# Global heads of an encoder trunk: groups of four query blocks, and softmax tiles shared by two blocks

## The chip, the cores and the metric

The kernel runs on one core of a Trainium2 chip. The core has a matrix engine (TensorE, in the profile PE, with its weight loads as a row of their own, PEld), three engines that work on rows of 128 partitions (VectorE or DVE, ScalarE or ACT, GpSimd or POOL), and an engine that here only issues transfers (SyncE or SP). Matmul results land in PSUM, a memory of eight banks of 128 partitions by 512 float32 columns; everything else lives in SBUF. The metric is the device time of one launch in microseconds, the median of several runs.

## The reference, cut to what matters

Two encoder layers of width 1024 over 1024 tokens. The first layer has three kinds of heads side by side; the change touches the kind with global attention, 8 query heads of width 64 that share 2 key and value heads.

```python
def global_gqa(q, k, v):
    ...
    scale = dh ** -0.5
    qb = q.reshape(B, nb, BLOCK, Hkv, G, dh).transpose(1, 0, 2, 3, 4, 5)

    def one(qblk):
        s = jnp.einsum('bqkgd,bskd->bkgqs', qblk, k).astype(jnp.float32) * scale
        p = jax.nn.softmax(s, axis=-1).astype(v.dtype)
        return jnp.einsum('bkgqs,bskd->bqkgd', p, v)
```

For each head and each block of 128 queries: the scores against all 1024 keys, a softmax along the keys, and the product with the values. Everything is float32.

## The kernel before, in words

**Stages.** One program does both layers. The first layer's attention (the phase `l0`) runs four passes; the method `even` calls `global_pair` once in each, at about 142 to 480 us of the span. A pass holds two query heads (`i` = 0, 1) of one key and value head, so 2 x 8 blocks of 128 queries. The other work of a pass is memory attention (`mem_att`) behind `global_pair`, and projections of the layer's input that later heads and the gate need.

**Numbers in two parts.** Matmul operands are rounded to a shorter form, and what rounding loses is carried in a second operand: a high and a low part. Keys come as `kh` and `kl`. A score tile takes four matmuls of 512 columns: two halves of the keys, each with `kh` and `kl` (L1046, L1047).

**A block's softmax.** `scores(i, g, b)` makes it: four matmuls into a PSUM tile `sa` of two banks (two such tiles, so two blocks at once); the maximum on DVE (L1051); on ACT one exponential of 1024 columns into an SBUF tile `P`, whose sum is accumulated on the way and fetched by a second small instruction (L1052); the reciprocal on DVE (L1053); and on POOL the multiplication by it (L1054). There are six `P` tiles of 128 x 1024.

**A group.** Two blocks of one head form a group (`g` = 0 to 3). Their weights stand with queries in the partitions, and must be turned so that keys do: PE transposes 128 x 128 pieces ("flips", L133) into a PSUM tile `tr`, four at a time, two key chunks of 128 of both blocks. `p_parts` takes the high part out on ACT (`ph`, L125) and the low part, the difference, on DVE (`pl`, L549). Four value matmuls of 256 columns follow (L1080): for each of the two chunks the high and the low part, all adding up in the one PSUM tile `pv`. That happens four times in a group (`c` = 0, 2, 4, 6). The values carry their own two parts in the upper and lower 64 output rows; at the group's end ACT copies the lower rows out (`bt`) and DVE adds both (L1086) into the pass's output `yb`.

**What lies between.** `pull(n)` issues steps of put-off projections: one step is three matmuls of 512 columns on one PSUM tile `pj` (L242). One step follows each set of flips, and four follow each of the pass's first two scores. So PE does the projections while ACT and DVE work on the softmax. `next(side)` issues other sums on POOL. New scores (`todo`) are begun ahead of chunks 0 and 4, so a pass is two blocks ahead of the flips.

**What sets the order.** The program text sets only dependencies and priorities. A scheduler with its own time model then orders each engine's instructions; `ahead(kind)` moves an instruction forward by the number of places given for `l0`: score=20, exp=60, part=150, close=120. The kinds `flip` and `pv` have no number there. On the chip each engine works through its own fixed list, and waits by semaphores. A tile with n buffers makes its n+1st writer wait for the last reader of the first: `P` has 6, `sa` 2, `tr` 2, `pv` 1, `pj` 1, `ph` and `pl` 3 each.

## Time and profile before

| what | us |
|---|---|
| median of 3 runs | 1479.58 (1479.55 to 1482.57) |
| profiled execution, its own time | 1482.22 |
| its span, first to last instruction | 1480.4 |
| mean granted TensorE clock | 0.998 |
| flips, all of the kernel (L133), x752 | 115.3 busy |
| exponentials of the global heads (L1052), x64 | 71.5 busy on ACT |
| maxima of the global heads (L1051), x64 | 77.5 busy on DVE |
| normalisations of the global heads (L1054), x64 | 73.8 busy on POOL |

The profile is of one execution. A row of a group names the line, the engine, the operation and the tiles (out<-in); then its count, its busy time, the mean length of one, and how long the engine stood idle before it with what ended that. A row of the timeline gives start and length in us, and in brackets how long the engine had waited and for what. Lengths of matmuls overlap, since PE starts one while the one before still drains: what a matmul costs is the step from its start to the next one's start, not its length. ACT and DVE rows overlap a little in the same way.

### The profile page before, as it was taken

What the parts mean: (1) busy time and instruction counts of PE and PEld (TensorE: products, weight loads), DVE (VectorE), ACT (ScalarE), POOL (GpSimd) and SP (SyncE); (2) the same over time, 40 slices, a digit from 0 to 9 for tenths busy, and PEclk for the clock granted to TensorE, in tenths of its full rate; (3) what the DMA queues carried; (4) which work ended last, traced back from release to release, by engine and by line L of the source; (5) the groups of instructions that cost most, each with busy time, mean ns of one, the idle gap of its engine ahead of it and who ended that gap; (6) DMA issues with size and microseconds to landing.
All of it is one profiled execution on the core that took longest, in us unless ns stands there. A gap on an engine that the chain in (4) does not pass through costs nothing.

```text
span 1480.4 us, 24751 instructions
## 1 busy us (share of the span) xinstructions
PE 1461.3 (99%) x8049; PEld 1254.1 (85%) x8049; DVE 1038.8 (70%) x2125; ACT 839.2 (57%) x1877; POOL 647.0 (44%) x766
## 2 busy tenths in 40 slices
PE   9999999999999999999999999999999999999997
PEld 8898888888888888888888887888888888888776
DVE  6687777777776678776687866654457787778584
ACT  7743665556655466655454544444456777776454
POOL 1223658566775656553450000002425556665355
PEclk9999999999999999999999999999999999999999
DMA  8966335334342524378553343567675568778844
GB/s 282 314 161 184 117 114 168 122 122 132 117 144 79 199 75 139 110 263 313 182 180 135 136 136 139 156 171 256 225 257 169 187 198 270 246 250 313 306 132 150
DMA packets 171809, 271.87 MB, mean 184 GB/s; under 512 B 15648, under 2 KB 92704, under 8 KB 170656
## 3 DMA queue, kind: packets, MB, share of 16 engines
q1 hardware_dynamic: 171248, 270.20, 56.6%
q8 instruction: 64, 1.05, 0.3%
q14 instruction: 65, 0.53, 0.1%
q10 hardware_dynamic: 432, 0.09, 0.0%
HBM read 174.28 MB, written 83.89 MB: 174 GB/s over the span
## 4 chain that ended last, share of the span: by engine, by line
PE 87%; DMA 4%; DVE 4%; ACT 2%; issue 1%; SPq 1%; POOL 0%; DVEq 0%; ACTq 0%; POOLq 0%
PE pj L242 16%; PE pj L62 12%; PE x L1650 7%; PE tr L133 6%; PE pv L1080 4%; PE y L1650 4%; PE pv L62 3%; PE s L62 3%; PE sa L1348 3%; PE tr L62 3%; PE pj L1348 2%; PE pv L1650 2%; PE sa L1046 2%; PE sa L1047 2%; PE s L1348 2%; PE tr L1348 2%
## 5 line engine op out<-in xcount | busy, mean ns | idle before, releaser
L549 DVE TENSOR_TENSOR pl<-tr,ph 128x512 fp32r<-128x512 f32 (+2 forms) x352 | 204.3, 594 | 45.2 <-ACT ph L125 43.3
L242 PE MATMUL pj<-H,wh 128*128 128x512 f32 x704 | 233.4, 412 | 0.4 <-DVE vt L313 0.2
L125 ACT ACTIVATE ph<-tr 128x512 fp32r<-128x512 f32 (+2 forms) x352 | 176.8, 523 | 99.6 <-PE tr L133 77.8
L158 POOL TENSOR_SCALAR wh<-wraw 128x512 fp32r<-128x512 f32 x48 | 30.4, 636 | 268.0 <-PE x L1650 233.2
L125 ACT ACTIVATE wh<-wraw 128x384 fp32r<-128x384 f32 (+1 forms) x163 | 89.2, 554 | 98.5 <-PE pj L1348 11.8
L242 PE MATMUL pj<-H,wl 128*128 128x512 f32 x352 | 139.0, 395 | 0.0
L242 PEld LDWEIGHTS pj<-H,wh 128*128 128x128 f32 x704 | 120.2, 189 | 18.2 <-issue 0.6
L62 PE MATMUL pj<-H,wh 128*128 128x512 f32 x384 | 121.0, 396 | 0.0
L1133 POOL TENSOR_SCALAR pn<-pn,st 128x384 f32<-128x384 f32 (+1 forms) x128 | 72.9, 572 | 99.3 <-DVE st L1132 57.5
L133 PE MATMUL tr<-ident,P 128*128 128x128 f32 x752 | 115.3, 273 | 0.8 <-DVE pl L549 0.5
L1295 POOL TENSOR_TENSOR wl<-wraw,wh 128x384 fp32r<-128x384 f32 x56 | 63.5, 1135 | 89.7 <-ACT wh L125 78.7
L1131 ACT ACTIVATE pn<-pn,st 128x384 f32<-128x384 f32 (+1 forms) x128 | 75.1, 587 | 40.4 <-DVE st L1128 38.9
L133 PEld LDWEIGHTS tr<-ident,P 128*128 128x128 f32 x752 | 88.8, 140 | 9.5 <-DVE pl L549 1.8
L1052 ACT ACTIVATE P<-sa,st 128x1024 f32<-128x1024 f32 x64 | 71.5, 1117 | 34.4 <-DVE st L1051 16.9
L1054 POOL TENSOR_SCALAR P<-P,st 128x1024 f32<-128x1024 f32 x64 | 73.8, 1155 | 27.5 <-DVE st L1053 27.2
L1051 DVE TENSOR_REDUCE st<-sa 128x1 f32<-128x1024 f32 x64 | 77.5, 1218 | 8.0 <-PE sa L1047 7.4
L62 PE MATMUL s<-k,q 128*128 128x384 f32 (+1 forms) x352 | 81.4, 327 | 0.7 <-DMA k<-k 0.7
L242 PEld LDWEIGHTS pj<-H,wl 128*128 128x128 f32 x352 | 66.2, 188 | 15.2
L62 PE MATMUL pj<-H,wl 128*128 128x512 f32 x192 | 75.6, 394 | 0.0
L160 POOL TENSOR_TENSOR wl<-wraw,wh 128x512 fp32r<-128x512 f32 x52 | 71.3, 1373 | 9.6 <-ACT wh L125 7.2
L62 PEld LDWEIGHTS pj<-H,wh 128*128 128x128 f32 x384 | 66.6, 188 | 5.4
L864 PE MATMUL pj<-ah,H 128*128 128x256 f32 x384 | 70.7, 282 | 0.3 <-ACT ah L125 0.2
(574 smaller groups left out, 4170.0 us busy)
## 6 DMA issues: line engine op xcount, KB each, us to landing
y<-yb SPq DMA_DIRECT2D x24, 512.0 KB, 3.9
wraw<-s SPq DMA_DIRECT2D x64, 192.0 KB, 3.8
wraw<-w_e SPq DMA_DIRECT2D x44, 256.0 KB, 3.5
k<-k SPq DMA_DIRECT2D x42, 256.0 KB, 5.5
s<-bias SPq DMA_DIRECT2D x56, 192.0 KB, 2.0
wq<-w_o SPq DMA_DIRECT2D x40, 256.0 KB, 3.3
y<-sg SPq DMA_DIRECT2D x18, 512.0 KB, 3.5
wraw<-w_o SPq DMA_DIRECT2D x36, 256.0 KB, 4.3
```

Source lines behind the costliest of these rows:

```text
L62: return lambda *a, **k: self.tc.keep_in_program_order(getattr(self.engine, name)(*a, **k))
L125: return self.nc.scalar.activation(out, in_, AF.Copy, scale=scale)
L133: self.turned = self.fence = self.pe.transpose(o, i, self.ident)
L242: self.pe.matmul(a[:, :n], s[:, kt % UNIT, :], m, start=(kt == 0 and i == 0), stop=(kt == KT - 1 and i == 2))
L549: self.low = nc.vector.tensor_tensor(pl[:, :n], tr[:, :n], ph[:, :n], op=OP.subtract)
L1051: nc.vector.tensor_reduce(st[:, 0:1], s, axis=AX.X, op=OP.max, negate=True)
L1052: nc.scalar.activation(pt, s, AF.Exp, bias=st[:, 0:1], accum_out=st[:, 1:2])
L1054: self.normal = nc.gpsimd.tensor_scalar(pt, pt, st[:, 2:3], 0.5, op0=OP.mult, op1=OP.mult)
L1131: nc.scalar.activation(o, o, AF.Exp, bias=st[:, 0:1], scale=-1.0, accum_out=st[:, 2:3])
L1133: self.normal = normal = nc.gpsimd.tensor_scalar(o, o, st[:, 3:4], 0.5, op0=OP.mult, op1=OP.mult)
L1348: last = nc.tensor.matmul(bank, s[:, k, :], y[3 * u + k][m][:, cols], start=start and u + k + e == 0, stop=u == 1 and k + e == 4, skip_gro ...
L1650: self.last = nc.tensor.matmul(bank, ws[s][:, k, :], b[k][m], start=start and k + i == 0, stop=k == UNIT - 1 and i == 2, skip_group_check= ...
```

## The change

A group now holds four query blocks of a head (`g` = 0, 1). The `P` tiles are still six of 128 x 1024, but one tile now holds the same half of the keys for two blocks, `[128, 2, 512]`: a pair of blocks takes two tiles. So a block's exponential is two ACT instructions of 512 columns, each with its own sum; DVE adds the two sums (L1057) and takes the reciprocal (L1058), and POOL normalises in two instructions. One set of four flips is now one key chunk of four blocks, and two value matmuls of 512 columns follow it (L1089). There are half as many group ends, each of 512 columns (L1094). At the head of a pass four blocks are begun, with two steps of projections behind each, where two blocks with four steps were. The numbers of score matmuls, flips, high and low parts, and projection steps stay.

```diff
         def scores(i, g, b):
-            qb = qs[i][:, (2 * g + b) * 128:(2 * g + b + 1) * 128]
+            blk = 4 * g + b
+            qb = qs[i][:, blk * 128:(blk + 1) * 128]
...
             st = self.tiny()
-            pt = self.st("P", [128, T])
+            if b % 2 == 0:
+                pts[i, g, b // 2] = [self.st("P", [128, 2, 512]) for _ in range(2)]
+            pt = [t[:, b % 2, :] for t in pts[i, g, b // 2]]
             with self.ahead("exp"):
                 nc.vector.tensor_reduce(st[:, 0:1], s, axis=AX.X, op=OP.max, negate=True)
-                nc.scalar.activation(pt, s, AF.Exp, bias=st[:, 0:1], accum_out=st[:, 1:2])
-                nc.vector.reciprocal(st[:, 2:3], st[:, 1:2])
-                self.normal = nc.gpsimd.tensor_scalar(pt, pt, st[:, 2:3], 0.5, op0=OP.mult, op1=OP.mult)
-            pts[i, g, b] = pt
-
-        todo = [(i, g, b) for i in range(2) for g in range(4) for b in range(2)]
-        for _ in range(2):
+                for k, t in enumerate(pt):
+                    nc.scalar.activation(t, s[:, k * 512:(k + 1) * 512], AF.Exp, bias=st[:, 0:1], accum_out=st[:, 1 + k:2 + k])
+                nc.vector.tensor_tensor(st[:, 3:4], st[:, 1:2], st[:, 2:3], op=OP.add)
+                nc.vector.reciprocal(st[:, 4:5], st[:, 3:4])
+                for t in pt:
+                    self.normal = nc.gpsimd.tensor_scalar(t, t, st[:, 4:5], 0.5, op0=OP.mult, op1=OP.mult)
+
+        def aside():
+            if todo:
+                with self.tc.issue_after(self.normal.ins):
+                    next(side, None)
+
+        todo = [(i, g, b) for i in range(2) for g in range(2) for b in range(4)]
+        for k in range(4):
             scores(*todo.pop(0))
-            self.pull(4)
+            if k > 1:
+                aside()
+            self.pull(2)
         for i in range(2):
-            for g in range(4):
+            for g in range(2):
                 p = [pts[i, g, b] for b in range(2)]
                 o = self.ps("pv")
-                for c in range(0, 8, 2):
-                    if c in (0, 4) and todo:
+                for c in range(8):
+                    if c % 2 == 0 and todo:
                         scores(*todo.pop(0))
-                        if todo:
-                            with self.tc.issue_after(self.normal.ins):
-                                next(side, None)
+                        aside()
                     tr = self.ps("tr")
                     with self.ahead("flip"):
-                        self.flip((tr[:, (2 * k + b) * 128:(2 * k + b + 1) * 128],
-                                   p[b][:, (c + k) * 128:(c + k + 1) * 128]) for k in range(2) for b in range(2))
+                        self.flip((tr[:, b * 128:(b + 1) * 128],
+                                   p[b // 2][c // 4][:, b % 2, c % 4 * 128:(c % 4 + 1) * 128]) for b in range(4))
                     parts = self.p_parts(tr, 512)
                     self.pull(1)
                     with self.ahead("pv"):
-                        for k in range(2):
-                            for part in parts:
-                                nc.tensor.matmul(o[:, :256], v[:, c + k, kv, :], part[:, k * 256:(k + 1) * 256],
-                                                 start=(c + k == 0 and part is parts[0]),
-                                                 stop=(c + k == 7 and part is parts[1]))
+                        for part in parts:
+                            nc.tensor.matmul(o, v[:, c, kv, :], part, start=c == 0 and part is parts[0],
+                                             stop=c == 7 and part is parts[1])
                 bt = self.st("bt", [64, 512])
                 with self.ahead("close"):
-                    self.copy(bt[:, :256], o[64:128, :256])
-                    nc.vector.tensor_tensor(y[64 * i:64 * i + 64, g * 256:(g + 1) * 256], o[0:64, :256], bt[:, :256],
-                                            op=OP.add)
+                    self.copy(bt, o[64:128, :])
+                    nc.vector.tensor_tensor(y[64 * i:64 * i + 64, g * 512:(g + 1) * 512], o[0:64, :], bt, op=OP.add)
```

Each engine's list of instructions is the scheduler's, so the diff alone does not tell it. Three places follow, each as it stood and as it stands. A row gives line, operation, out<-in and the shape; the number behind a tile's name tells its instances apart, and `x2` means two alike in a row.

**ACT in the middle of a group, first pass.** Before, from the exponential (`P`) that waits for the flips into `tr_2485`, to the end of the group (`bt`):

```order
L1052 ACTIVATE P_2614,st_2613<-sa_2608,st_2613 128x1024
L125 ACTIVATE ph_2490<-tr_2485 128x512
L1052 ACTIVATE P_2661,st_2660<-sa_2655,st_2660 128x1024
L125 ACTIVATE ph_2524<-tr_2519 128x512
L125 ACTIVATE bt_2501<-pv_2392 64x256
```

The change, from the first half exponential that waits for the flips into `tr_2406`:

```order
L1056 ACTIVATE P_2434,st_2433<-sa_2428,st_2433 128x512
L1056 ACTIVATE P_2434,st_2492<-sa_2487,st_2492 128x512
L125 ACTIVATE ph_2411<-tr_2406 128x512
L1056 ACTIVATE P_2435,st_2433<-sa_2428,st_2433 128x512
L1056 ACTIVATE P_2435,st_2492<-sa_2487,st_2492 128x512
L443 ACTIVATE sg_2123<-vt_2418 128x512
L125 ACTIVATE ph_2451<-tr_2446 128x512
```

Where a whole block, a copy and a whole block stood, the first halves of two blocks now stand ahead of the copy and their second halves behind it. The score tile `sa_2428` is read to its end by the third of these exponentials, not by the first.

**PE at the same place.** Before, right behind the flips into `tr_2485` and the three projection matmuls that follow them, to the next score (`sa_2708`):

```order
L1080 MATMUL pv_2392<-ph_2474,va_145 128x256
L1080 MATMUL pv_2392<-pl_2475,va_145 128x256
L1080 MATMUL pv_2392<-ph_2474,va_145 128x256
L1080 MATMUL pv_2392<-pl_2475,va_145 128x256
L133 MATMUL tr_2519<-ident_63,P_2399 128x128
L133 MATMUL tr_2519<-ident_63,P_2458 128x128
L133 MATMUL tr_2519<-ident_63,P_2399 128x128
L133 MATMUL tr_2519<-ident_63,P_2458 128x128
L242 MATMUL pj_2428<-H_122,wh_2424 128x512
L242 MATMUL pj_2428<-H_130,wh_2424 128x512
L242 MATMUL pj_2428<-H_122,wl_2425 128x512
L1046 MATMUL sa_2708<-k_137,q_144 128x512
```

The change, right behind the flips into `tr_2406` and the three projection matmuls that follow them, to the next score (`sa_2534`), which takes the buffer of `sa_2428`:

```order
L1089 MATMUL pv_2232<-ph_2397,va_145 128x512
L1089 MATMUL pv_2232<-pl_2398,va_145 128x512
L133 MATMUL tr_2446<-ident_63,P_2239 128x128 x2
L133 MATMUL tr_2446<-ident_63,P_2333 128x128 x2
L242 MATMUL pj_2467<-H_118,wh_2457 128x512
L242 MATMUL pj_2467<-H_126,wh_2457 128x512
L242 MATMUL pj_2467<-H_118,wl_2458 128x512
L1089 MATMUL pv_2232<-ph_2411,va_145 128x512
L1047 MATMUL sa_2534<-k_137,q_144 128x512
```

The score keeps its place behind two sets of flips and two steps of projections; the value matmuls in between are three of 512 columns where four of 256 were, and the flips' set `tr_2446` already belongs to the next group.

**DVE where a group ends.** Before, around the closing add (L1086) of the group whose sum is `pv_2289`; `sg` is a gate product, `vt` its factor:

```order
L1053 RECIPROCAL st_2510<-st_2510 128x1
L444 SCALAR_TENSOR_TENSOR sg_2123<-sg_2123,vt_2381 128x512
L549 TENSOR_TENSOR pl_2413<-tr_2407,ph_2412 128x512
L1051 TENSOR_REDUCE st_2613<-sa_2608 128x1
L1053 RECIPROCAL st_2556<-st_2556 128x1
L1086 TENSOR_TENSOR yb_2122<-pv_2289,bt_2389 64x256
L549 TENSOR_TENSOR pl_2442<-tr_2436,ph_2441 128x512
L1051 TENSOR_REDUCE st_2660<-sa_2655 128x1
```

The change, around the closing add (L1094) of the sum `pv_2232`:

```order
L1058 RECIPROCAL st_2492<-st_2492 128x1
L1054 TENSOR_REDUCE st_2539<-sa_2534 128x1
L444 SCALAR_TENSOR_TENSOR sg_2123<-sg_2123,vt_2418 128x512
L549 TENSOR_TENSOR pl_2452<-tr_2446,ph_2451 128x512
L1094 TENSOR_TENSOR yb_2122<-pv_2232,bt_2424 64x512
L549 TENSOR_TENSOR pl_2479<-tr_2473,ph_2478 128x512
L1054 TENSOR_REDUCE st_2585<-sa_2580 128x1
```

The maximum of a score now stands ahead of the gate product and of the low part of the next group's first flips; before, it stood behind both.

**PE at the head of the first pass.** Before, the first two scores stand together and 24 projection matmuls follow; then come the third score (`sa_2190`) and the fourth, and the first flips. In the change, 12 projection matmuls follow the first two, and then comes the third (`sa_2179`, its last matmul is the first row; the two rows `tr_2251` and `tr_2266` are first pieces of the first two sets of flips):

```order
L1048 MATMUL sa_2179<-k_138,q_143 128x512
L242 MATMUL pj_2153<-H_122,wh_2149 128x512
L242 MATMUL pj_2153<-H_130,wh_2149 128x512
L242 MATMUL pj_2153<-H_122,wl_2150 128x512
L242 MATMUL pj_2153<-H_123,wh_2149 128x512
L242 MATMUL pj_2153<-H_131,wh_2149 128x512
L242 MATMUL pj_2153<-H_123,wl_2150 128x512
L133 MATMUL tr_2251<-ident_63,P_2132 128x128
L133 MATMUL tr_2266<-ident_63,P_2132 128x128
L1047 MATMUL sa_2203<-k_137,q_143 128x512
```

Behind the fourth score (`sa_2203`) stand six more projection matmuls, two more flips, the fifth (`sa_2233`) and sixth (`sa_2280`) scores, two flips, and the seventh (`sa_2327`). The 24 projection matmuls that stood between the second and the third score are now spread from the second to the fifth.

## The prediction

> **What bounds the kernel now.** First the page: share of the span by engine, then the chain that ended last.
>
> ```profile
> span 1480.4 us, 24751 instructions
> PE 1461.3 (99%) x8049; PEld 1254.1 (85%) x8049; DVE 1038.8 (70%) x2125; ACT 839.2 (57%) x1877; POOL 647.0 (44%) x766
> ```
>
> TensorE (PE) is busy all along, but the modelled ends of its matmuls overlap, so "busy" hides short stalls. Second, the waits of PE between 140 and 505 us, which hold every global head:
>
> ```profile
> PE tr L133 <- DVE pl L549: 0.5, 1, 0.5
> PE tr L133 <- DVE vt L311: 0.2, 1, 0.2
> PE pj L242 <- DVE vt L331: 0.2, 1, 0.2
> ```
>
> 0.9 us in 365. Third, one 40 us stretch (columns: length, then PE, weight loads, DVE, ACT, POOL busy):
>
> ```profile
> 260.00:300.00 40.00, 40.00 (x269) 36.02 (x268) 28.12 (x48) 24.57 (x52) 20.51 (x27) 1.00 0.37 115
> ```
>
> PE sets the time here, at full clock, with DVE at 70% and ACT at 61%. So PE has nothing to gain from others; it can only do less, or begin to wait. Fourth, the groups of that stretch that the change touches:
>
> ```profile
> L1080 PE MATMUL pv<-ph,va 128*128 128x256 f32 x256 | 66.2, 283 | 0.0
> L1080 PE MATMUL pv<-pl,va 128*128 128x256 f32 x256 | 65.2, 282 | 0.0
> L1052 ACT ACTIVATE P<-sa,st 128x1024 f32<-128x1024 f32 x64 | 71.5, 1117 | 34.4 <-DVE st L1051 16.9 <-PE tr L133 16.4 <-POOL bias L1278 0.9
> L1051 DVE TENSOR_REDUCE st<-sa 128x1 f32<-128x1024 f32 x64 | 77.5, 1218 | 8.0 <-PE sa L1047 7.4 <-POOL P L665 0.5
> L1054 POOL TENSOR_SCALAR P<-P,st 128x1024 f32<-128x1024 f32 x64 | 73.8, 1155 | 27.5 <-DVE st L1053 27.2
> ```
>
> The exponentials already wait for PE's flips (16.4 us): a P tile is free only once its last block is flipped.
>
> **Change, part 1: wider value matmuls.** 512 matmuls of 256 columns become 256 of 512. A matmul's cost is the step from start to start (PE rows of the timeline):
>
> ```profile
> 250.21 0.40 PE L1046 MATMUL sa<-k,q 128*128 128x512 f32 x1
> ...
> 252.06 0.28 PE L1080 MATMUL pv<-ph,va 128*128 128x256 f32 x1
> ...
> 252.53 0.60 PE L133 MATMUL tr<-ident,P 128*128 128x128 f32 x4
> ...
> 253.66 0.28 PE L1080 MATMUL pv<-ph,va 128*128 128x256 f32 x1
> ```
>
> Eight score matmuls of 512 columns stand between 250.21 and 252.06: 1.85/8 = 0.231 us each. Four value matmuls stand between 252.06 and 252.53: 0.1175 each. Before 512 x 0.1175 = 60.2 us, after 256 x 0.231 = 59.2: **-1.0 us**, on PE's path in full. (From 252.53 to 253.66 there are four flips and three projection matmuls; less 3 x 0.231, the four flips take 0.44.) The closing copy and add halve in number off that path.
>
> **Part 2: halves of a block, shared by two blocks.** Six P buffers stay; four hold the group that is being flipped, so two serve the blocks to come. The rows of order show the result: the next two blocks' first halves wait for the flips of chunk 3 (or 7) of the group, and ACT runs half, half, copy of the flips, half, half. A score tile is free only after both halves of its block, and the next score stands on PE at a fixed place behind those flips: four flips, three projections, two value matmuls, four flips, three projections, one value matmul, that is 0.44 + 0.69 + 0.46 + 0.44 + 0.69 + 0.23 = 2.95 us. I count 19 such places (5, 4, 5 and 5 in the four passes). Is the score released by then? The same place before, in the timeline (start, length, then in brackets the wait and what ended it):
>
> ```profile
> 262.49 0.60 PE L133 MATMUL tr<-ident,P 128*128 128x128 f32 x4
> 263.06 1.11 ACT L1052 ACTIVATE P<-sa,st 128x1024 f32<-128x1024 f32 x1 [1.42 <-PE tr L133]
> 264.08 0.19 ACT L1052 ACTIVATION_READ_ACCUMULATOR P<-sa,st 128x1 f32 x1
> 264.17 0.59 ACT L125 ACTIVATE ph<-tr 128x512 fp32r<-128x512 f32 x1
> 264.65 1.12 ACT L1052 ACTIVATE P<-sa,st 128x1024 f32<-128x1024 f32 x1
> 265.23 0.39 PE L1046 MATMUL sa<-k,q 128*128 128x512 f32 x1
> ```
>
> An exponential's read with a score waiting behind it, a copy that waits for the fourth of the flips of 252.53 above, and, from another stage, exponentials of 256 columns:
>
> ```profile
> 158.27 0.20 ACT L1052 ACTIVATION_READ_ACCUMULATOR P<-sa,st 128x1 f32 x1
> ...
> 158.53 0.19 PEld L1046 LDWEIGHTS sa<-k,q 128*128 128x128 f32 x1
> 158.75 0.40 PE L1046 MATMUL sa<-k,q 128*128 128x512 f32 x1
> ...
> 253.22 0.60 ACT L125 ACTIVATE ph<-tr 128x512 fp32r<-128x512 f32 x1 [2.85 <-PE tr L133]
> ...
> 1029.40 0.47 ACT L2127 ACTIVATE k<-s,st 128x256 f32<-128x256 f32 x1
> 1029.76 0.20 ACT L2127 ACTIVATION_READ_ACCUMULATOR k<-s,st 128x1 f32 x1
> 1029.86 0.47 ACT L2127 ACTIVATE k<-s,st 128x256 f32<-128x256 f32 x1
> ```
>
> Delays: ACT starts 0.57 us after the first flip if it needs the third flip (262.49 to 263.06), 0.69 if it needs the fourth (252.53 to 253.22), so about 0.45 for the second, which frees the first of two tiles. An exponential of 1024 columns with its read takes 1.02 + 0.09 = 1.11 until the next may start; of 256 columns 0.36 + 0.10 = 0.46. Between them 512 columns take 0.36 + 0.66/3 = 0.58, with the read 0.67; to the read's end 0.58 + 0.20 = 0.78. A copy takes 0.48 (264.17 to 264.65). From the read's end to the score matmul 0.28 (158.47 to 158.75).
>
> Before: 0.57 + 1.02 + 0.19 + 0.28 = 2.06 us after the flips; the score stood at 2.74 and never waited. After: 0.45 + 0.67 + 0.67 + 0.48 + 0.78 + 0.28 = 3.33, the place is 2.95: **0.38 us of stall, 19 times, 7.2 us**. Ends: if a half costs just half a block (0.51 + 0.09), 3.12 and 0.17, 3.2 us in all; if the first half needs the fourth flip, 0.62 and 11.8 us; nothing, if the halves end 0.13 earlier each. I take the middle, since the interpolation stands between two rows of the same operation.
>
> **Part 3: where a group ends.** At eight places (two a pass) DVE now does the maximum of the first of the two scores, then a gate product, then the low part of the new group's first flips; before, gate and low part stood ahead of the maximum. The group's third flips need that low part, to reuse its PSUM buffer, and no value matmul stands between, since the sum's only bank is still being closed.
>
> ```profile
> 151.24 0.39 PE L1047 MATMUL sa<-k,q 128*128 128x512 f32 x1
> ...
> 151.66 1.22 DVE L1051 TENSOR_REDUCE st<-sa 128x1 f32<-128x1024 f32 x1 [0.22 <-PE sa L1047]
> 152.80 0.68 DVE L444 SCALAR_TENSOR_TENSOR sg<-sg,vt 128x512 f32<-128x512 f32 x1
> 152.92 1.12 ACT L1052 ACTIVATE P<-sa,st 128x1024 f32<-128x1024 f32 x1 [0.81 <-DVE st L1051]
> 153.40 1.22 DVE L1051 TENSOR_REDUCE st<-sa 128x1 f32<-128x1024 f32 x1
> ```
>
> And a flip that waits for a low part now:
>
> ```profile
> 259.56 0.68 DVE L549 TENSOR_TENSOR pl<-tr,ph 128x512 fp32r<-128x512 f32 x1
> ...
> 260.38 0.63 PE L133 MATMUL tr<-ident,P 128*128 128x128 f32 x4
> ```
>
> DVE, counted from the score's end (151.24 + 0.23): 0.19 + 1.14 (maximum to gate) + 0.60 (gate to next) + 0.68, and 0.14 to the flip (260.24 to 260.38) = 2.75. PE there: value matmul 0.23, flips 0.44, projections 0.69, second score 0.92 = 2.28. **0.47 us, 8 times, 3.8 us.** Nothing at the low end, if the gate's factor comes so early that DVE is free for it sooner; the order forbids more than 0.60 of that.
>
> **Part 4: the head of a pass.** Four blocks, not two, go through the softmax before the first flips. Passes 1 and 3 have memory attention around them as cover; 0 and 2 do not.
>
> ```profile
> 144.90 0.70 PE L242 MATMUL pj<-H,wh 128*128 128x512 f32 x2
> ...
> 146.20 1.28 ACT L1052 ACT_TABLE_LOAD   x1 [2.27 <-DMA wraw<-w_e]
> ...
> 147.49 1.12 ACT L1052 ACTIVATE P<-sa,st 128x1024 f32<-128x1024 f32 x1
> ...
> 150.55 0.39 PE L1046 MATMUL sa<-k,q 128*128 128x512 f32 x1
> ```
>
> In pass 0 the third score stood behind 24 projection matmuls, at 150.55; now it stands behind 12, at 144.90 + 12 x 0.235 = 147.7. It needs the first block's exponentials, from 147.49 (behind a table load): 147.49 + 0.67 + 0.78 + 0.28 = 149.2. **1.5 us**, once. Then, in passes 0 and 2, the sixth and seventh scores stand too near those whose buffer they take. From a score's end to its buffer's next matmul: 0.19 + 1.26 (151.66 to 152.92) + 0.67 + 0.78 + 0.28 = 3.18. The sixth score follows the fourth's end by six projections, two flips and a score, 1.39 + 0.22 + 0.92 = 2.53: 0.65 of stall. The seventh follows the fifth's end by that stall, a score and two flips, 1.79: 1.39. **2 x 2.0 = 4.1 us.** Low end: nothing, if PE is late there for other reasons.
>
> POOL's normalisation doubles in number, 64 more fixed costs; POOL has half its time free and the flips come later than its halves, so I count nothing; were the cover gone, the flips would wait for it.
>
> **Sum.** -1.0 + 7.2 + 3.8 + 1.5 + 4.1 = +15.6 us. The profiled execution's own time is 1482.2 us (1.8 around its span) and would be 1497.8; it lies 2.6 above the median of the runs, 1479.6, so the forecast is **1495 us**. The terms' ends give 1478.6 (no stall) to some 1502.
>
> **Rivals.** (a) No stall shows: the halves are done a little sooner than interpolated and PE's places are late enough, as they were before with 0.68 us to spare. Only part 1 remains: 1478.6, no change. Against: the spare is used up by two more halves ahead of the one that counts. [...] 17%.
>
> (b) Wide value matmuls gain more. Each one has its own weight load, and loads are busy 36.0 of 40 us; if loads and not columns set the step, a wide matmul could cost its load alone, 36.02 us/268 = 0.134, and 256 of them 34.3: -25.9 us, and with parts 2 to 4 about 1470. Against: score matmuls of this very width step by 0.231. [...] 7%.
>
> (c) ACT falls behind for good: it does 64 x (2 x 0.67 - 1.11) = 15 us more, and where each first half waits for the fourth flip the 19 stalls are 11.8 us: 1500. For: the exponentials wait for flips already. Against: ACT has 39% free. 10%.
>
> **Numbers.** Forecast 66%, (a) 17, (b) 7, (c) 10. 0.2%, 3.0 us, is what a measurement of this kernel can tell from no change: faster 9% ((b) and the edge of (a)), the same 16%, slower 75%. Range 1478 to 1502: from (a) to (c) and a little beyond.
>
> **What would show it.** After: PE waits "sa <- ACT P" some 19 times and "tr <- DVE pl" 8 times; a stall shows some 0.16 smaller there, as modelled ends overlap. Half exponentials near 0.69 us and copies at 0.60; value matmuls at a step of 0.231; the third score of pass 0 near 149.2; the last score of the global heads (446 now) some 15 later. Wrong if scores follow the previous matmul by 0.23 throughout: then parts 2 to 4 fall together.

## The result, and the profile after

The changed kernel takes **1499.04 us** (median of 5 runs, 1499.01 to 1501.66) against 1479.68 before (5 runs, 1479.55 to 1483.59): ratio **1.0122**, 95% interval 1.011 to 1.0135, 19.4 us slower. The forecast was 1495, range 1478 to 1502.

The first lines of its page:

```profile
span 1499.3 us, 24472 instructions
PE 1469.3 (98%) x7793; PEld 1236.3 (82%) x7793; DVE 1057.6 (71%) x2173; ACT 849.4 (57%) x1989; POOL 664.4 (44%) x830
```

PE has 256 instructions fewer than before. Where the time went is seen best in the global heads alone. I measure them from the first score matmul to the 661st of the projection matmuls of L242, which both kernels have: this **stage** took 347.4 us before. Busy time in it before (columns: length, PE, weight loads, DVE, ACT, POOL, clock, DMA share, GB/s):

```profile
142.80:490.20 347.40, 346.89 (x2095) 303.94 (x2094) 252.26 (x388) 209.35 (x417) 223.55 (x272) 1.00 0.41 130
```

and after:

```profile
143.70:508.50 364.80, 355.52 (x1839) 285.58 (x1838) 267.47 (x438) 221.35 (x529) 240.27 (x334) 1.00 0.39 124
```

The stage is 17.4 us longer. The other 1.5 us of the span lie ahead of it (0.9, where PE's list is the same) and behind it (0.6). Both parts vary by more than that between kernels that leave them alone: in the profiles of the twelve runs below, the first score stood at 141.0 to 146.2 us, and what lies behind the stage, up to the last matmul, took 981.5 to 987.3 us. So the stage is the measure in what follows, beside the whole time.

PE was busy for all but 0.5 us of its stage before; now 9.3 us are open idle time, and its modelled busy time grew by 8.6 with 256 matmuls fewer, which are steps stretched by waits. What PE waited for between 140 and 520 us (total, times, longest):

```profile
PE sa L1047 <- ACT P L1056: 4.7, 5, 1.8
PE tr L133 <- DVE pl L549: 3.7, 8, 0.8
PE pj L242 <- DVE vt L313: 0.6, 1, 0.6
```

The first row is scores that wait for exponentials, the second flips that wait for a low part, eight times, as many as there are group ends of this kind. Modelled ends hide the shorter waits, so I also took PE's steps, start to start, and set each against its usual length. The groups of the changed part, in the same stage:

```profile
L1089 PE MATMUL pv<-ph,va 128*128 128x512 f32 x128 | 51.1, 399 | 0.0
L1056 ACT ACTIVATE P<-sa,st 128x512 f32<-128x512 f32 x128 | 86.9, 689 | 27.7 <-PE tr L133 16.8 <-DVE st L1054 10.8
L125 ACT ACTIVATE ph<-tr 128x512 fp32r<-128x512 f32 x143 | 85.4, 600 | 80.2 <-PE tr L133 79.8
L444 DVE SCALAR_TENSOR_TENSOR sg<-sg,vt 128x512 f32<-128x512 f32 x16 | 12.7, 791 | 0.4
L1060 POOL TENSOR_SCALAR P<-P,st 128x512 f32<-128x512 f32 x128 | 95.9, 764 | 44.0 <-DVE st L1058 30.5 <-ACT ph L125 7.7 <-ACT P L1056 2.4
```

POOL's normalisation rose from 73.8 to 95.9 us of busy time for the same numbers, in twice as many instructions.

**The score place.** One of them in the timeline of the change (start, length, in brackets the wait):

```profile
166.87 0.60 PE L133 MATMUL tr<-ident,P 128*128 128x128 f32 x4
167.33 0.69 ACT L1056 ACTIVATE P<-sa,st 128x512 f32<-128x512 f32 x1 [0.60 <-PE tr L133]
...
169.15 0.69 ACT L1056 ACTIVATE P<-sa,st 128x512 f32<-128x512 f32 x1
...
169.61 0.39 PE L1089 MATMUL pv<-ph,va 128*128 128x512 f32 x1
169.72 0.21 ACT L1056 ACTIVATION_READ_ACCUMULATOR P<-sa,st 128x1 f32 x1
...
169.99 0.50 PE L1047 MATMUL sa<-k,q 128*128 128x512 f32 x1
...
170.32 0.39 PE L1048 MATMUL sa<-k,q 128*128 128x512 f32 x1
```

The first half starts 0.46 us after the flips, the third half 1.82 later, and the score stands 0.38 behind the value matmul instead of 0.23. It starts 0.27 after the read of the exponential's sum began, which is 0.05 after the read ended. The trace shows what releases the score tile: the exponential itself raises no semaphore, the read does, 0.01 after its end. Behind the wait the score's own step is 0.33 instead of 0.23.

**The group end**, in the same view:

```profile
179.78 1.22 DVE L1054 TENSOR_REDUCE st<-sa 128x1 f32<-128x1024 f32 x1
180.92 0.68 DVE L444 SCALAR_TENSOR_TENSOR sg<-sg,vt 128x512 f32<-128x512 f32 x1
181.52 0.69 DVE L549 TENSOR_TENSOR pl<-tr,ph 128x512 fp32r<-128x512 f32 x1
181.56 0.40 PE L1048 MATMUL sa<-k,q 128*128 128x512 f32 x1
182.35 0.63 PE L133 MATMUL tr<-ident,P 128*128 128x128 f32 x4 [0.40 <-DVE pl L549]
```

Maximum, gate product and low part follow each other without a gap; the flips start 0.79 us after the last score matmul instead of 0.23.

**The head of pass 0**, likewise:

```profile
147.81 1.28 ACT L1056 ACT_TABLE_LOAD   x1 [2.99 <-DMA wraw<-w_e]
148.44 0.40 PE L242 MATMUL pj<-H,wl 128*128 128x512 f32 x1
149.11 0.69 ACT L1056 ACTIVATE P<-sa,st 128x512 f32<-128x512 f32 x1
150.61 0.50 PE L1047 MATMUL sa<-k,q 128*128 128x512 f32 x1 [1.77 <-ACT P L1056]
151.93 1.05 PE L242 MATMUL pj<-H,wh 128*128 128x512 f32 x2
```

The third score waits. The two projection matmuls at 151.93 take 0.43 each and not 0.23, and the window from 151.5 to 154.5 shows why, in its clock column:

```profile
151.50:154.50 3.00, 3.00 (x9) 2.21 (x8) 1.46 (x3) 1.47 (x5) 1.67 (x4) 0.50 0.90 336
```

PE ran at half its clock, by the trace's clock records from 151.31 for 3.41 us.

The account of the stage, from the steps:

| part | forecast, us | measured, us |
|---|---|---|
| value matmuls (512 x 0.1187 before, 256 x 0.2324 after) | -1.0 | -1.3 |
| scores that wait for exponentials, in the groups | 7.2 (19 places) | 1.6 (10 places of 0.15 to 0.16) |
| flips behind a group end (8) | 3.8 | 5.0 (0.55 to 0.97 each) |
| third score of pass 0 | 1.5 | 1.9 |
| half clock behind it | none | 1.4 |
| sixth and seventh scores, passes 0 and 2 | 4.1 | 1.7 + 2.2 |
| a projection behind DVE at the head of pass 3 | none | 0.8 |
| projections that wait for their PSUM tile (10) | none | 1.3 |
| left over, by difference: mostly steps stretched by up to 0.1 us right behind a wait | none | 2.8 |
| sum | 15.6 | 17.4 |

### The profile page after: what moved, and what is told of

Same layout as the page of the kernel before. It is cut to its first block, busy times and chain, and to the rows that moved or that the text cites. A ratio compares the mean times of both kernels' runs of the same rounds, so it can differ in the third digit from the quotient of the medians.

```text
span 1499.3 us, 24472 instructions
## 1 busy us (share of the span) xinstructions
PE 1469.3 (98%) x7793; PEld 1236.3 (82%) x7793; DVE 1057.6 (71%) x2173; ACT 849.4 (57%) x1989; POOL 664.4 (44%) x830
## 4 chain that ended last, share of the span: by engine, by line
PE 67%; DVE 4%; ACT 2%; issue 2%; DMA 1%; POOL 1%; DVEq 0%; ACTq 0%; POOLq 0%; SPq 0%
PE pj L62 12%; PE pj L242 9%; PE x L1657 6%; PE y L1657 4%; PE pv L62 3%; PE s L62 3%; PE tr L133 3%; PE tr L62 3%; PE pj L1355 3%; PE sa L1355 2%; PE pv L1657 2%; PE s L1355 2%; PE tr L1355 2%; PE pv L1089 2%; PE pv L757 1%
## 5 line engine op out<-in xcount | busy, mean ns | idle before, releaser
L242 PE MATMUL pj<-H,wh 128*128 128x512 f32 x704 | 236.1, 416 | 1.1 <-DVE vt L313 0.8
L242 PE MATMUL pj<-H,wl 128*128 128x512 f32 x352 | 139.8, 397 | 0.0
L242 PEld LDWEIGHTS pj<-H,wh 128*128 128x128 f32 x704 | 120.5, 191 | 20.3 <-DVE vt L313 1.6
L133 PEld LDWEIGHTS tr<-ident,P 128*128 128x128 f32 x752 | 92.6, 140 | 29.3 <-PE sa L1048 7.0
L1060 POOL TENSOR_SCALAR P<-P,st 128x512 f32<-128x512 f32 x128 | 95.9, 764 | 44.0 <-DVE st L1058 30.5
L1056 ACT ACTIVATE P<-sa,st 128x512 f32<-128x512 f32 x128 | 86.9, 689 | 27.7 <-PE tr L133 16.8
L242 PEld LDWEIGHTS pj<-H,wl 128*128 128x128 f32 x352 | 66.5, 189 | 15.3
```

The costliest lines, as they stand in the source:

```text
L133: self.turned = self.fence = self.pe.transpose(o, i, self.ident)
L242: self.pe.matmul(a[:, :n], s[:, kt % UNIT, :], m, start=(kt == 0 and i == 0), stop=(kt == KT - 1 and i == 2))
L1056: nc.scalar.activation(t, s[:, k * 512:(k + 1) * 512], AF.Exp, bias=st[:, 0:1], accum_out=st[:, 1 + k:2 + k])
L1060: self.normal = nc.gpsimd.tensor_scalar(t, t, st[:, 4:5], 0.5, op0=OP.mult, op1=OP.mult)
```

## The experiments

All are edits of the changed kernel, but the first. "Stage" is the one above: 347.4 us before, 364.8 in the change's first profile.

| run | median, us | ratio to before, 95% interval | stage, us |
|---|---|---|---|
| the change | 1499.04 | 1.0122 (1.011 to 1.0135) | 364.8 |
| e1 halves alone | 1484.05 | 1.0012 (1.0002 to 1.0022) | 349.5 |
| e2 narrow values | 1496.97 | 1.0104 (1.0089 to 1.0119) | 363.6 |
| e3 scores later | 1523.54 | 1.028 (1.0263 to 1.0296) | 391.9 |
| e4 sink load early | 1500.95 | 1.0125 (1.0108 to 1.0142) | 361.3 |
| e5 gate on POOL | 1490.9 | 1.0064 (1.0049 to 1.0079) | 358.6 |
| e6 exponentials ahead | 1504.45 | 1.0155 (1.0138 to 1.0172) | 371.1 |
| e7 whole blocks | 1495.77 | 1.0095 (1.0075 to 1.0116) | 361.1 |
| e8 three mends | 1501.09 | 1.0134 (1.0119 to 1.0149) | 360.3 |
| e9 the change again | 1499.32 | 1.0122 (1.0105 to 1.0139) | 362.8 |
| e10 narrow values again | 1498.39 | 1.0114 (1.0095 to 1.0133) | 364.2 |
| e11 whole blocks again | 1495.33 | 1.0092 (1.0076 to 1.0107) | 361.6 |
| e12 whole blocks, gate on POOL | 1510.58 | 1.0194 (1.0178 to 1.021) | 377.7 |

The kernel before took 1482.32 us beside e1 to e4, 1482.07 beside e5 to e8 and 1481.14 beside e9 to e12.

### e1: the halves alone, in groups of two

```diff
 # in the kernel before
-            pt = self.st("P", [128, T])
+            if b == 0:
+                pts[i, g] = [self.st("P", [128, 2, 512]) for _ in range(2)]
+            pt = [t[:, b, :] for t in pts[i, g]]
...
-                nc.scalar.activation(pt, s, AF.Exp, bias=st[:, 0:1], accum_out=st[:, 1:2])
+                for k, t in enumerate(pt):
+                    nc.scalar.activation(t, s[:, k * 512:(k + 1) * 512], AF.Exp, bias=st[:, 0:1], accum_out=st[:, 1 + k:2 + k])
```

> The kernel before with one part of the change alone: groups of two blocks and value matmuls of 256 columns stay, but the two blocks of a group share two P tiles by halves of the keys, so each exponential, and each normalisation, is two instructions of 512 columns. Theory (the loss comes from the order that groups of four with six P tiles force: half, half, copy, half, half between the flips of chunk 3 or 7 and the next score): here only two of six P tiles hold the group being flipped, so four serve the blocks to come and the exponentials wait less for flips; the place before had 0.68 us to spare and a block's two halves with reads take 1.35 where a whole took 1.11. No stalls on PE: 1479.6, at most 1482. Rival (halves themselves are the cause, by 15 us more work on ACT and 64 more fixed costs on POOL): 1487 or more.

Measured: 1.7 us above before, within the theory's bound. One score waits, 0.1 us at the head of pass 0; the others don't. The main new wait is small, five times 0.2 us, a value matmul behind the closing sum (here its weight load, which stands in front of it):

```profile
192.94 0.19 PEld L1084 LDWEIGHTS pv<-ph,va 128*128 128x128 f32 x1 [0.47 <-DVE yb L1090]
```

So halves as such are not the cause; they cost in the order that groups of four give.

### e2 and e10: narrow value matmuls in the changed kernel

```diff
-                            nc.tensor.matmul(o, v[:, c, kv, :], part, start=c == 0 and part is parts[0],
-                                             stop=c == 7 and part is parts[1])
+                            first = c == 0 and part is parts[0]
+                            for h in range(1 if first else 2):
+                                m = slice(0, 512) if first else slice(h * 256, (h + 1) * 256)
+                                nc.tensor.matmul(o[:, m], v[:, c, kv, :], part[:, m], start=first,
+                                                 stop=c == 7 and part is parts[1] and h == 1)
```

> The changed kernel with its value matmuls cut to 256 columns again (only the first of each group keeps 512 columns, since it opens the sum): 248 matmuls more. Theory (a value matmul costs its columns, 0.1175 us for 256 and 0.231 for 512): 248 x 0.004 = 1.0 us more, part of which falls into stalls that are there anyway: 1499.0 to 1500.1. [...]

> The changed kernel with value matmuls of 256 columns (the first of each group excepted), as before, now beside the change itself. Theory (a value matmul costs its columns): 0 to 1.0 us more than the change, and the 2.7 us less that stood between the two ratios was the half clock, missing in the one profile, and the spread of the runs. Rival (narrow matmuls let the closing work or the low parts start sooner, and are better in this structure): 2 to 3 us less than the change.

> The changed kernel itself, on the same chip and in the same rounds as the three below, so that they can be compared. 18 to 20 us above the kernel before. If the half clock at the head of pass 0 follows from the stall of about 2 us there (theory), it may be there or not from one execution to the next, worth 1.4 us; everything else in the global heads is as in the first profile (364.8 us from the first score to the 661st projection matmul of the stage, with or without these 1.4).

In e2 the median stood 2.1 us below the change's, from other rounds. Side by side (e9, e10) the two are 0.9 apart with intervals that overlap: no difference that the runs can tell. The stages are 364.2 narrow and 362.8 wide; of the 1.5 between them, 0.3 is a longer wait of the third score and 0.5 a longer one at the head of pass 3, which leaves 0.7 for 248 matmuls more. A value matmul steps by 0.2324 us with 512 columns and by 0.119 (median) with 256. Rival (b) of the prediction, a gain of wide matmuls beyond their columns, is out here too: 0.2324 is 0.006 less than two narrow steps. Why e2's median was lower is not shown. In the profiles its stage is 1.3 us shorter than the change's first one, about what the half clock cost there: it is missing in e2, and in e9 as well, at the very place:

```profile
149.55 0.50 PE L1047 MATMUL sa<-k,q 128*128 128x512 f32 x1 [1.45 <-ACT P L1056]
149.88 0.39 PE L1048 MATMUL sa<-k,q 128*128 128x512 f32 x1
```

(e2; the wait is 1.45 where the change's first profile had 1.77.)

### e3: the scores a chunk later

```diff
-                    if c % 2 == 0 and todo:
-                        scores(*todo.pop(0))
+                    if c % 4 > 1 and todo:
+                        with self.tc.issue_after(self.turned.ins):
+                            scores(*todo.pop(0))
                         aside()
```

> The changed kernel with the next two scores of each half group put behind the flips of chunks 1 and 2 (or 5 and 6) instead of 0 and 1 (4 and 5). From the flips of chunk 3 or 7 to the next score PE then has some 3.6 to 3.9 us of work instead of 2.95, ACT does a block's two halves without a copy in between, and the maximum no longer stands ahead of the low part at a group's end. Theory (the score places and group ends are the stalls that count, some 11 of the 17 us lost in the global heads; the rest is the heads of passes 0 and 2): 1487 to 1490. Rival (ACT or DVE are short of time as such, so the stall only moves to another place): 1496 or more.

The waits that it was to remove are gone from the groups, and larger ones took their place. PE's waits in e3 (total, times, longest):

```profile
PE tr L133 <- POOL P L1060: 19.2, 16, 2.0
PE pj L242 <- DVE vt L313: 3.0, 1, 3.0
PE pv L1090 <- DVE yb L1095: 2.9, 4, 0.7
PE pv L1090 <- DVE pl L549: 2.3, 8, 0.3
```

With the scores a chunk later, the normalisation on POOL ends after PE comes to flip its tile, 16 times. The theory's number falls, and the rival's bound (1496 or more) is far exceeded; but the engine that was late is POOL, which neither had named. The scores stand between two limits: earlier, they wait for exponentials; later, the flips wait for POOL. Part of the loss came behind the waits: five stretches of half clock follow them (the mean granted clock of the profiled execution is 0.992, against 0.997 in the change's), which at the 1.4 us that one cost in the change is an estimated 7 of the 27 us.

### e4: the sink load out of ACT's queue

```diff
-        sink = self.st("sink", [128, 8])
+        sink = self.st("sink", [128, 8], pool=self.base)
```

> The changed kernel with one small load moved: the sink logits (128 x 8) get a place of their own in SBUF, so their transfer is issued at the start of the program and not from ACT's queue at the head of pass 0, where ACT stood from 144.8 to 147.8 behind it, ahead of its table load and the first exponentials. Theory (the third score's stall of 1.94 us at the head of pass 0 is this wait; the half clock from 151.4 to 154.5, ten steps of 0.43 instead of 0.23, follows from that stall): the first exponential some 2.4 us earlier, no stall there, no half clock: 3.4 us less than the change, some 1495.6. Rival 1 (the half clock has another cause, the DMA load for one): 1.9 us less and the clock drops as before, 1497.1. Rival 2 (ACT waits for something else): 1499.

At the head of pass 0 it did what the theory said (timeline of e4):

```profile
145.57 1.28 ACT L1056 ACT_TABLE_LOAD   x1
146.05 0.39 PE L1048 MATMUL sa<-k,q 128*128 128x512 f32 x1
147.55 0.69 ACT L1056 ACTIVATE P<-sa,st 128x512 f32<-128x512 f32 x1 [0.70 <-DVE st L1054]
149.41 0.40 PE L1047 MATMUL sa<-k,q 128*128 128x512 f32 x1
```

No wait of the third score, no half clock, and the stage is 3.5 us shorter (3.4 expected) than in the change's first profile, 1.4 shorter than in e9, which had the wait and no half clock. The whole time did not follow: 1500.95, the same as the change. The load's wait had moved to another engine. The instruction that uses the sink logits, on DVE, stood at 150.9 us in the change; it now stands at the start of the program and waits there for the same load (timeline of e4):

```profile
8.57 0.17 DVE L1948 TENSOR_SCALAR sink<-sink 128x8 f32<-128x8 f32 x1 [3.03 <-DMA sink<-sink_b]
```

PE waits 2.6 us for a DVE result behind it, and its granted clock is half from 8.6 to 12.0 us. PE's 61st matmul starts at 15.7 us instead of 12.7; apart from e8, which has the load moved too (16.7), no profile is later than 12.9. Other work makes up for most of it, and the stage begins 0.7 us later than in the change's first profile, 3.4 later than in e9. What follows it took 987.3 us instead of 983.7 (985.6 in e9), spread over layer 1; why is open.

### e5: the gate product on POOL

```diff
+            if self.raw:
+                nc.gpsimd.tensor_scalar(sg[:, c:c + n], sg[:, c:c + n], 1.0, None, op0=OP.add)
+                nc.gpsimd.tensor_tensor(sg[:, c:c + n], sg[:, c:c + n], p[:, :n], op=OP.mult)
+            else:
                 nc.vector.scalar_tensor_tensor(sg[:, c:c + n], sg[:, c:c + n], 1.0, p[:, :n], op0=OP.add, op1=OP.mult)
```

> The changed kernel with the gate product of layer 0 (one DVE instruction of 512 columns) done by two instructions on POOL, so that at a group's end the maximum is followed at once by the low part. PE's order is the same but for one place. Theory (DVE's chain from the score's end to the flips is what the third flips of a group wait for): the chain is 2.75 - 0.60 = 2.15 us and PE's work there 2.28, so the eight stalls of 0.55 to 0.97 go, with the slow restart behind each: 5 to 6 us less from the first score to the end of the global heads, 1493 to 1494. Rival 1 (the flips wait as much for ACT's closing copy): half of it at most, 1496.5 or more. Rival 2 (POOL's two gate instructions delay the normalisations, and flips wait for those): 1499 or more.

PE's waits in the stage of e5:

```profile
PE sa L1051 <- ACT P L1060: 4.5, 5, 1.6
PE pj L242 <- DVE vt L313: 0.9, 1, 0.9
PE tr L133 <- DVE pl L553: 0.5, 1, 0.5
```

Of eight waits for the low part one is left. The same place in its timeline: the low part follows the maximum at once, and the flips follow the last score matmul by 0.23.

```profile
176.63 1.23 DVE L1058 TENSOR_REDUCE st<-sa 128x1 f32<-128x1024 f32 x1
177.77 0.68 DVE L553 TENSOR_TENSOR pl<-tr,ph 128x512 fp32r<-128x512 f32 x1
178.42 0.40 PE L1052 MATMUL sa<-k,q 128*128 128x512 f32 x1
178.65 0.60 PE L133 MATMUL tr<-ident,P 128*128 128x128 f32 x4
```

The stage is 6.3 us shorter than in the change's first profile and 4.2 shorter than in e9, which had no half clock; e5 had none either. So 4 to 5 us are the group ends, and this part of the prediction is shown. The whole time gained more, to 8.8 us above before; the rest of it lies outside the stage, within its spread.

### e6: exponentials ahead of the copies

```diff
-    "l0": dict(sink=300, score=20, exp=60, part=150, close=120),
+    "l0": dict(sink=300, score=20, exp=160, part=150, close=120),
```

> The changed kernel with one number of the order table changed: exp=160 instead of 60 for the global heads. ACT then does half, half, half, copy, half, so the first of the two scores is released after three halves and no copy: 0.45 + 0.68 + 0.68 + 0.57 + 0.27 = 2.65 us after the flips, and PE's order, which follows, has 2.72 us of work there. Theory (score places wait for this chain): the ten waits of 0.15 us at the scores go with the slow restart behind each, some 3 us; at a group's end PE has 0.2 us more work ahead of the third flips, 1.6 us in eight: 1494 to 1496. Rival (the high part that the copy makes is now what is late, value matmuls wait for it): 1499 or more.

PE's waits in the stage of e6:

```profile
PE tr L133 <- POOL P L1060: 4.5, 5, 2.0
PE sa L1047 <- ACT P L1056: 4.5, 5, 1.5
PE tr L133 <- DVE pl L549: 3.5, 8, 0.9
PE pv L1089 <- DVE yb L1094: 2.4, 8, 0.3
```

The score places still wait, eight times 0.14 us instead of ten times 0.15, so the 0.07 us that I had put to spare weren't there. The group ends still wait for the low part, value matmuls now wait eight times for the closing sum, and flips five times for POOL: 6.2 us more in the stage. The rival's sign was right, its reason not: the copies were not what came late.

### e7, e11: whole blocks in groups of four

```diff
-            if b % 2 == 0:
-                pts[i, g, b // 2] = [self.st("P", [128, 2, 512]) for _ in range(2)]
-            pt = [t[:, b % 2, :] for t in pts[i, g, b // 2]]
+            pts[i, g, b] = pt = self.st("P", [128, T])
...
+                nc.scalar.activation(pt, s, AF.Exp, bias=st[:, 0:1], accum_out=st[:, 1:2])
+                nc.vector.reciprocal(st[:, 2:3], st[:, 1:2])
+                self.normal = nc.gpsimd.tensor_scalar(pt, pt, st[:, 2:3], 0.5, op0=OP.mult, op1=OP.mult)
```

> The changed kernel with the halves undone: groups of four blocks and value matmuls of 512 columns stay, but each block has one P tile of 128 x 1024 again and one exponential. Four of six tiles are held until the flips of chunk 7; only then can the third and fourth block of the next group be computed. Theory (P tiles set when exponentials start): behind chunk 7 two exponentials, a reciprocal and a normalisation in a row, 0.45 + 1.11 + 1.11 + 0.35 + 1.15 = 4.2 us, against some 3.5 of PE's work, and again for the next scores: 1 to 2 us at each of 12 changes of group above what the change has: 1500 to 1520. Rival (the halves don't help groups of four, they only cost): 1494 or less.

> The changed kernel with one exponential and one P tile for each block (groups of four, value matmuls of 512 columns), beside the change itself. Theory (from the profile of its first run, 361.1 us in the global heads against 364.8): the halves cost this structure some 4 us, 14 to 16 us above the kernel before. Rival (the first run's two times were a chance): as slow as the change, 18 or more above.

My theory for e7 was wrong. Four of six tiles held until chunk 7 cost no more than the halves do: the waits that I had priced at 1 to 2 us for each change of group are these, from PE's waits in e7,

```profile
PE pv L1084 <- DVE yb L1089: 2.4, 4, 0.6
PE tr L133 <- POOL P L1055: 2.3, 8, 0.8
PE pv L1084 <- DVE pl L549: 1.3, 7, 0.2
```

6.0 us in all. The scheduler puts the next scores right behind the flips of chunk 7, where they cover the exponentials. Beside the change (e9) whole blocks were 4.0 us faster by the medians; the intervals of the two ratios just touch, and the stages are 1.1 us apart (361.6 and 362.8). So in groups of four halving the blocks gains nothing; that it costs some 4 us is likely, not shown. And groups of four with whole blocks are still 14.2 us above before (e11), so most of the change's loss comes with the groups of four, halves or not.

### e8 and e12: mends together

e8 is e4, e5 and e6 in one kernel, e12 is e7 with the gate product on POOL.

> The changed kernel with three mends together: the sink load early (its tile with a place of its own), the gate product on POOL, and exp=160. Theory (the change's loss is stalls at places of their own, so the mends add up): 3.4 + 5.5 + 3 us less than the change, and what is left are the heads of passes 0 and 2 (0.4 + 1.3 and 2.2 us), 0.8 at the head of pass 3 and 1.3 where projections wait for their PSUM tile: 1487. Rival (a mended place hands its stall on to the next one): 1492 or more.

> Whole blocks, and the gate product on POOL instead of DVE: the two single edits that gained, together. Theory (at a change of group DVE is late with the low parts and the closing sum, 3.7 us of PE's waits in the profile of whole blocks): 3 to 5 us less than whole blocks alone, some 10 us above the kernel before, and still not faster than it, since wide value matmuls have only 1 us to give. Rival (POOL, for whose normalisation flips wait 2.3 us there already, becomes what is late): no gain or a loss against whole blocks alone.

Neither adds up. e8's stage, 360.3 us, is longer than e5's alone (358.6), and the waits for the closing sum that e6 has and e5 has not are there again, 1.2 us; its first score stood at 146.2 us, 2.5 later than in the change, and as in e4 DVE waits for the moved load at the start, 3.9 us. In e12 the rival decides, by PE's waits:

```profile
PE tr L133 <- POOL P L1059: 17.8, 18, 2.8
PE pv L1088 <- DVE pl L553: 1.0, 3, 0.6
```

But the gate's two instructions are not what stands in the way: in none of the 18 places are they among what POOL did without a break ahead of the late normalisation. There the scheduler's order has put side sums (`bias`) and the splitting of weights (`wh`, `wl`). In the place shown here, from POOL's timeline in e12 ahead of a flip at 174.63 that waited 1.9 us, a side sum had itself waited for a load:

```profile
170.49 0.60 POOL L1283 TENSOR_TENSOR bias<-bias 128x192 f32<-128x192 f32 x1 [4.95 <-DMA bias<-w_oe]
...
173.46 1.12 POOL L1059 TENSOR_SCALAR P<-P,st 128x1024 f32<-128x1024 f32 x1
```

Two stretches of half clock (357.3 to 364.1 and 469.9 to 473.3 us) add to the loss. No kernel of the study comes below the one before; with 1.3 us to gain from the value matmuls, none of them could have by more than that.

## Why the prediction was right, and where it was not

**What bounds the kernel.** Right: PE had no time to gain from others, only to lose. The group ends are shown as a cause by e5, and the load as the cause of the third score's wait by e4. For the score places no experiment took the wait away (e6 was to); they rest on the trace.

**Part 1** held: -1.3 us by the steps against -1.0, and e9 beside e10 shows no more. Rival (b) is out: loads don't set the step, a wide matmul cost 0.232 us.

**Part 2** had the mechanism and missed the size, 1.6 us in place of 7.2 (2.6 with the slow step behind each wait). The step that failed is "from the read's end to the score matmul 0.28": the score started 0.05 us after the read's end, so 0.22 of the 0.38 us of stall never was. The row that I had taken for it (a score at 158.75 behind a read that ended at 158.47) was a score that did not wait at all: it stood 0.23 behind the matmul in front of it. The interpolated half was right (0.66 to 0.68 to the next start measured, 0.67 put), and so were the copy (0.48) and the start behind the flips (0.46, put 0.45). The second error is the count: one of the 19 places waited 0.1 us only, and eight did not show a wait, for at these PE had been held up some 0.14 us just before, when a projection waited for DVE to empty its one PSUM tile. Before, a score stood between two such projections and covered this; I had costed what the new order puts behind the flips, and not what it takes away from in front of the projections.

**Part 3** held: 5.0 us against 3.8, seven of the eight between 0.55 and 0.68 instead of 0.47.

**Part 4** held: the third score waited 1.9 us (1.6 in e9) instead of 1.5, the sixth and seventh 0.4 and 1.3 in pass 0 (put 0.65 and 1.39) and 2.2 together in pass 2 (put 2.04). The 0.22 us too much of part 2 stood in the sixth score's wait as well: without it the two come to 0.43 and 1.39. That half clock would stand behind the wait, 0.50 for 3.41 us in the change's first profile, I had not seen coming. Nor the 0.8 us at the head of pass 3.

**POOL at nothing** was true of this kernel and close to false: e3 and e12 show 19.2 and 17.8 us of flips that wait for POOL after small moves. "POOL has half its time free" was the wrong measure. What counted was how long before the flips its last half is done.

**Sum.** 15.6 forecast, 17.4 in the stage, 19.4 in the medians. The sum came out nearer than its terms: 5.6 us too much for the score places stood against 1.2 too little for the group ends and some 6 us of costs that I had not listed (half clock, projections, slow restarts, pass 3). That these nearly cancel is luck. The upper end was added up wrongly: 1502 starts from the profiled execution's 1482.2; from the median the terms' ends give 1479.6 + 20.2 = 1499.8, which 1499.04 only just meets. Rival (a), no stall, is out by the waits; of (c), ACT behind for good, there is no sign: ACT waits 16.8 us for flips in the stage, as it did before.

## What to carry to other kernels

Where one engine is busy all the time, a change that regroups its work is priced by the order that comes out, not by the instructions saved: for each place where it meets another engine, count the work between the release and the use, before and after, in both directions. A place that "has time to spare" has it because of what stands in front of it, so ask of each moved piece what it used to cover. And an engine at 44% can be the next to decide when its results are due at a fixed moment: look at the time between its last result and the first use.

## What the runs showed of the hardware

**The clock.** Behind some of its longer waits PE ran at half its clock. In the change's first profile the third score's start lies 2.17 us behind the start in front of it (148.44 to 150.61), and from 151.31 to 154.72 us the steps are 0.427 instead of 0.232 us with 512 columns, with a granted clock of 0.50 in the row above. At the same place in e2 the two starts lie 1.83 us apart (147.72 to 149.55), and no half clock followed. Between 130 and 520 us the fourteen profiles have eleven places where two PE starts lie 2.17 to 3.4 us apart; six were followed by it and five were not. Single ones of 1.8 to 2.1 us never were, five in all; but in e3 two close together (1.76 and 1.60) were, and in e12 several shorter ones. In e3 the half clock begins at 150.19, 160.43, 180.91, 273.07 and 447.15 us. So in these runs the length of a single wait did not tell whether half clock followed.

**The restart.** A score that had to wait was followed by the next matmul of 512 columns after 0.33 us instead of 0.23 (169.99 to 170.32 above; the same in e2, 149.55 to 149.88). Such a wait costs PE 0.1 us more than its length. Right behind a set of flips a matmul of 512 columns takes 0.31 to 0.32 without any wait, and with one 0.33 to 0.34: there a wait adds 0.02.

**The release.** An exponential with an accumulated sum is two instructions, and its PSUM tile is free when the second, the read of the sum, ends: in the change's profile the waiting matmul starts 0.05 us after the read's end, 0.25 to 0.27 after its start, twelve times.
